# Encoder block on one core: earlier weights for the first two gates, and another PSUM bank for one fill

## Chip, core and metric

The kernel runs on one NeuronCore of one Trainium2 chip. The metric is the device time of one execution in microseconds (us). Five instruction streams run beside each other on the core and meet only at semaphores: PE (TensorE, matmuls), DVE (VectorE), ACT (ScalarE), POOL (GpSimd) and SP (SyncE, which issues most DMAs). PE writes its results to PSUM, which has 8 banks of 128 x 512 float32; DVE and ACT read them there. Everything else is in SBUF.

## What is computed

One encoder block over 1024 positions and 1024 channels, float32. From the normalised input come, by one projection, the queries, keys and values, two gate paths, and the inputs u and v of a gated MLP. Attention and MLP are two branches; each is projected back to 1024 channels, and two sigmoid gates made from the input weigh them against each other.

```python
h = rmsnorm(x, norm_gain)
z = jnp.einsum('bsd,de->bse', h, w_in)
q, k, v, gate_a, u_in, v_in, gate_b, g_merge = jnp.split(z, IN_SPLITS, axis=-1)
...
attn = block_attention(q, k, v) * jax.nn.silu(gate_a)
y_a = jnp.einsum('bse,ed->bsd', attn, w_proj_attn)
...
gm = u * v_mix.reshape(B, S, GMLP_WIDTH) * jax.nn.silu(gate_b)
y_b = jnp.einsum('bse,ed->bsd', gm, w_proj_gmlp)
g = jax.nn.sigmoid(g_merge.reshape(B, S, N_BRANCHES, D_MODEL) + b_merge)
y = g[:, :, 0, :] * y_a + g[:, :, 1, :] * y_b
return x + jnp.einsum('bsd,de->bse', y, w_out)
```

A final rmsnorm follows. There are 8 query heads and 2 key/value heads of 64, so the attention has 64 score tiles of 128 queries x 1024 keys.

## The kernel before

Most matrices are split into a high and a low part, and a product is three matmuls (high by high, high by low, low by high). A weight tile arrives by DMA ("wraw"), ACT makes the high part ("wh", line 110) and DVE or POOL the low part ("wl", line 116).

The order of the program is: keys and values; v of the MLP and its position mixing; queries; the attention with the remaining projections as filling work; the projection of the MLP branch, `proj_b`, here called the spatial projection (product "yb", eight output tiles `dt`); the eight pairs of merge gates `g0` to `g7` and, between them, the projection of the attention, `a0` to `a3`; the output projection.

The code is written in program order, without waits. A scheduler then sets the fixed order of each engine from that order and from when buffers come free, so a line that moves in the program can move instructions on every engine, and each engine runs its own list strictly in order. Buffers come from tags with a fixed number of slots: a new tile of a tag takes the slot of the oldest one and waits for its last reader. Three tags matter here. In PSUM there are three tiles of two banks ("S", for scores and large products), one bank "o" (`ps_o`) and one bank "z" (`ps_z`). In SBUF the tag "t2" (line 57) has four buffers of 128 x 512 float32.

The attention (lines 534 to 626). `scores` (line 545) makes a score tile on PE (s, lines 550 and 551), its negated maximum on DVE (nm, 553), the exponentials on ACT (P, 557), and splits the result into two float16 parts (p, ACT 563, DVE 564), which a transposing DMA turns (T, line 567). `mix` (line 569) multiplies the values with T in bank "o" (o, line 575); ACT and DVE add the halves (o2, line 578; og, 582). Between them stand the fills: 24 half tiles of the gate and u projections, of 24 matmuls each. Fill `fill_u` (507) has DVE read its bank (uw, line 511), then a tanh form of gelu (ut, 274 to 277), and POOL multiplies it into vm (514); `fill_a` (524) has DVE read it at line 494 (product ga, tile ga00w). `fill_bank` (line 503) chooses the bank of a fill: the n-th entry of `FB`, and "z" after that. The first two fills are u2's halves, `u20` and `u21`, the third is the first half of a0, `ga00`. Two of four groups of query transposes (qtp, line 349, copied by ACT at line 351 to qT) fall between the first fills, and those of rows 2 and 3 use "o" as well (`QTP`, line 354).

The gates (lines 666 to 720 and 807 to 832). `pair_weights` loads the weights of one gate pair ("graw", 1 MB), takes the squares of its four quarters on ACT (line 814; the squares themselves go to `junk`, which is bank "o"; their sums are kept), makes a scale of them (`unit_scale`, 666 to 675, with PE at 669, POOL at 673) and forms three sums on DVE (`sums`, 714 to 716, two of them in new tiles s1 and s2 of tag "t2"). `pair` then makes the product by seven instead of eight half products (`seven`, 683 to 711): "11", "21", "T2", "T3", "T1", "22", "T4", each with weights split by ACT (line 680) and DVE (681), 12 matmuls each into the first bank of a tile "S". The first product is copied by ACT to p1 (a "t2" tile, line 700), and DVE adds the others to it (696). The other operand are forms of the input (xf, from `x_chunk`) and, for `a0` to `a3`, of the attention (gf, gk), made by ACT and DVE at lines 110, 116 and 652.

`MORDER` (line 736) is the order of the last stage: "w" is `pair_weights`, "g" is `pair`, "a" a pair of output tiles of the attention's projection, "A" makes its forms.

Of the kernel before, what the change touches and what calls it, by code (L numbers as in the profile page):

```python
# [30 lines left out]
def hybrid_block_kernel(  # L31
# [30 lines left out]
    def junk(name):  # L62
        return ps_o(name)
# [13 lines left out]
    def ps_z(name):  # L77
        return ps.tile([P, 512], F32, tag="z", bufs=1, name=name)
# [99 lines left out]
    for i in range(4):  # L178
        for j in range(2):
            dt = 2 * i + j  # L180
# [11 lines left out]
            for tt in range(NT):  # L192
                o = kvb[tt // 2][:, 256 * (tt % 2):256 * (tt % 2) + 256]
# [303 lines left out]
        dve.scalar_tensor_tensor(out=t, in0=t, scalar=1.0, in1=w, op0=ALU.add, op1=ALU.mult)  # L497
        return t

    FB = (ps_z,)  # L500
    nfill = []

    def fill_bank(name):
        nfill.append(name)
        return FB[len(nfill) - 1](name) if len(nfill) <= len(FB) else ps_z(name)

# [124 lines left out]
    def proj_b(dt):  # L631
        yp = ps_s(f"yb{dt}")
        hi, lo = stream_w(W_PROJ + dt, 1, act, dve)
        for h in range(2):
            for et in range(4):
                mm3(yp[:, H(h)], hi[:, C(et)], lo[:, C(et)], gmh[:, et, H(h)], gml[et][:, H(h)], et == 0, et == 3)
        act.copy(ys[dt], yp)
# [95 lines left out]
    XLO = (dve, dve)  # L733
    XCS = (0, 1, 3, 5)
    EARLY = 2
    MORDER = "w0 g0 w1 g1 w2 A a0 g2 w3 g3 w4 a1 g4 w5 g5 w6 a2 g6 w7 a3 o g7"

    gk = []

# [12 lines left out]
    def load_chunk(j):  # L752
        for dt in (j, j + 4):
            xraw[dt] = t4(XT[j], f"xraw{dt}")
            nc.sync.dma_start(out=xraw[dt], in_=xT[C(dt), :])

    def x_chunk(j):
        q = {}
        for r in range(2):
            dt = j + 4 * r  # L760
            for h in range(2):
                t = q[r, h] = xraw[dt][:, None, H(h)]
                dve.scalar_tensor_tensor(out=xraw[dt][:, H(h)], in0=xraw[dt][:, H(h)], scalar=gs[:, dt:dt + 1],
                                         in1=rB[:, H(h)], op0=ALU.mult, op1=ALU.mult)

        def xf_tile(key, i):
            if not xfn:
                tag = XFT.pop(0)
                if tag == "ptr":
                    t = sb.tile([P, 4, 2, 1, 512], F16, tag="ptr", bufs=2, name=f"xf{key}{j}")  # L770
                else:
                    t = t4(tag, f"xf{key}{j}", F16, (P, 2048)).rearrange("p (n f k t) -> p n f k t", n=2, f=2, k=1)
                xfn.extend(t[:, n] for n in range(t.shape[1]))
            t = xfn.pop(0)
            return t[:, 0], t[:, 1]

        make_forms(q, 1, xf_tile, XB, XSUB, XHI, XLO)

    for j in range(2):
        load_chunk(j)  # L780
    for dt in range(8):
        proj_b(dt)
        if dt in XCS:
            j = XCS.index(dt)
            x_chunk(j)
            if j + 2 < 4:
                load_chunk(j + 2)

    def halves_of(t):
        return [t[:, H(0)], t[:, H(1)]]  # L790
# [16 lines left out]
    def pair_weights(dt):  # L807
        t = t8("qT", 4, f"graw{dt}", F32)
        nc.sync.dma_start(out=t[:, 0, :], in_=wall[W_TR + 20 + dt])
        nc.sync.dma_start(out=t[:, 1, :], in_=wall[W_TR + 12 + dt])  # L810
        a21, a22, a11, a12 = (t[:, k, H(h)] for k in range(2) for h in range(2))
        ss = small(f"gss{dt}", 4)
        for i, t in enumerate((a21, a22, a11, a12)):
            act.activation(junk(f"gsq{dt}{i}"), t, AF.Square, accum_out=ss[:, i:i + 1])
        sc = unit_scale(ss, 4, f"g{dt}")
        return sums(a11, a12, a21, a22, t2(f"s1{dt}"), t2(f"s2{dt}")), sc
# [20 lines left out]
        dve.tensor_tensor(out=ys[dt], in0=ys[dt], in1=ga, op=ALU.add)  # L837

    gates, GA, pws, yas = {}, {}, {}, {}
    yhl, who = {}, []  # L840

    wor, who4 = [], []
# [38 lines left out]

    for step in MORDER.split():
        i = int(step[1:] or 0)
# [149 lines left out]
```

## Time and profile before

| | us |
|---|---|
| median of 3 runs (lowest, highest) | 746.56 (745.75, 747.24) |
| the profiled execution | 744.79 |
| its span | 743.0 |
| PE busy | 712.1 |
| DVE busy | 596.4 |
| ACT busy | 446.8 |
| POOL busy | 97.2 |

The mean granted TensorE clock of the profiled execution is 0.988 of full speed. A row of the trace gives the start and duration of an instruction, its engine, line, operation and tiles, and in brackets how long its engine had nothing to do before it and which instruction ended that. Matmuls overlap, so their spacing is read from their starts. Where the chain of waits names several, it is the last to come.

### The profile page before, as it was taken

How to read it: one execution, taken by the hardware profiler on the slowest of the kernel's cores; microseconds unless marked ns; L12 is line 12 of the kernel's file. 1: busy time of each engine (PE TensorE's matmuls, PEld its weight loads, DVE VectorE, ACT ScalarE, POOL GpSimd, SP SyncE). 2: the span in 40 equal slices, each digit the busy share in tenths (PEclk: the TensorE clock that was granted, in tenths of full speed). 3: DMA queues.
4: the chain of work that ended last, by engine and by line, in shares of the span. 5: the costliest groups of instructions: out<-in, count | busy, mean ns of one | idle time of the engine just before them, and what ended most of it. 6: DMA issues, size and time to landing. Idle time of an engine off the chain costs nothing.

```text
span 743.0 us, 9814 instructions
## 1 busy us (share of the span) xinstructions
PE 712.1 (96%) x3561; PEld 530.1 (71%) x3561; DVE 596.4 (80%) x931; ACT 446.8 (60%) x775; POOL 97.2 (13%) x77
## 2 busy tenths in 40 slices
PE   8999999988999999999999995999999998999995
PEld 8978888766778888888878882455464555588884
DVE  5568988789798999988899999899888899934223
ACT  6646664676788898768787488555474446611101
POOL 0010242142121321232200002000000000000000
PEclk9999999989999999999999998999999999999998
DMA  8831301083769897898999800130031006241111
GB/s 309 301 100 36 114 15 42 1 142 78 136 128 181 166 179 142 162 177 157 166 234 323 183 16 1 56 128 15 18 125 57 0 1 231 109 142 68 46 58 56
DMA packets 152609, 85.47 MB, mean 115 GB/s; under 512 B 135408, under 2 KB 136048, under 8 KB 152560
## 3 DMA queue, kind: packets, MB, share of 16 engines
q1 hardware_dynamic: 152272, 84.56, 45.7%
q8 instruction: 28, 0.46, 0.3%
q10 hardware_dynamic: 288, 0.28, 0.1%
q14 instruction: 21, 0.17, 0.1%
HBM read 47.07 MB, written 4.19 MB: 69 GB/s over the span
## 4 chain that ended last, share of the span: by engine, by line
PE 81%; DVE 9%; DMA 4%; ACT 2%; issue 2%; POOL 1%; SPq 0%; POOLq 0%; DVEq 0%; ACTq 0%
PE o L575 6%; PE out L174 4%; PE out L173 4%; PE out L172 4%; DMA T<-p 3%; PE s L550 3%; PE s L551 3%; PE g L172 3%; PE g L174 3%; PE g L173 3%; PE q L172 2%; PE q L174 2%; PE v L172 2%; PE q L173 2%; PE v L173 2%; PE v L174 2%
## 5 line engine op out<-in xcount | busy, mean ns | idle before, releaser
L564 DVE SCALAR_TENSOR_TENSOR p<-P,ri,p 128x1024 f16<-128x1024 f32 x64 | 88.9, 1393 | 14.7 <-ACT p L563 14.3
L557 ACT ACTIVATE P<-s,nm 128x1024 f32<-128x1024 f32 x64 | 71.4, 1116 | 23.0 <-DVE nm L553 11.5
L553 DVE TENSOR_REDUCE nm<-s 128x1 f32<-128x1024 f32 x64 | 77.8, 1215 | 5.7 <-PE s L551 5.4
L563 ACT ACTIVATE p<-P,ri 128x1024 f16<-128x1024 f32 x64 | 72.8, 1143 | 14.7 <-DMA T<-p 11.3
L575 PE MATMUL o<-T,vS 128*128 128x256 f16 x512 | 61.8, 273 | 2.1 <-DMA T<-p 2.1
L575 PEld LDWEIGHTS <-vS 128*128 128x128 f16 x512 | 47.4, 98 | 16.0 <-issue 6.9
L550 PE MATMUL s<-kT,qT 128*128 128x512 f32 x128 | 53.0, 414 | 1.3 <-ACT P L557 1.3
L116 POOL TENSOR_TENSOR wl<-wraw,wh 128x512 fp32r<-128x512 f32 x24 | 36.0, 1504 | 111.6 <-ACT wh L110 96.2
L551 PE MATMUL s<-kT,qT 128*128 128x512 f32 x128 | 50.5, 395 | 0.0
L909 ACT ACTIVATE sq<-xr 128x1024 f32<-128x1024 f32 x7 | 7.4, 1061 | 61.5 <-DVE xr L963 61.5
L963 DVE TENSOR_TENSOR xr<-out,xr 128x1024 f32<-128x1024 f32 x7 | 8.6, 1225 | 44.0 <-PE out L174 43.9
L673 POOL TENSOR_TENSOR scg<-scg,mhalf 128x1 f32<-128x1 f32 x8 | 9.8, 1219 | 221.6 <-DVE scg L672 221.6
L110 ACT CAST wh<-wraw 128x512 fp32r<-128x512 f32 x35 | 21.5, 614 | 17.5 <-PE yb L173 7.5
L488 PE MATMUL ga<-xh,wh 128*128 128x512 f32 x64 | 26.5, 414 | 3.8 <-DVE uw L511 3.4
L550 PEld LDWEIGHTS s<-kT,qT 128*128 128x128 f32 x128 | 24.1, 188 | 6.7 <-ACT P L557 1.9
L551 PEld LDWEIGHTS s<-kT,qT 128*128 128x128 f32 x128 | 24.1, 188 | 4.9 <-issue 0.2
L488 PE MATMUL u<-xh,wh 128*128 128x512 f32 x64 | 25.6, 399 | 0.7 <-DVE ga01w L494 0.7
L490 PE MATMUL ga<-xh,wl 128*128 128x512 f32 x64 | 26.1, 407 | 0.0
L489 PE MATMUL ga<-xl,wh 128*128 128x512 f32 x64 | 26.0, 406 | 0.0
L680 ACT ACTIVATE wg<-graw,scg 128x512 f16<-128x512 f32 x16 | 11.4, 721 | 24.2 <-PE g L174 12.8
L172 PE MATMUL v<-nh,xh 128*128 128x512 f32 x64 | 25.5, 398 | 0.0
L174 PE MATMUL yb<-gmh,wl 128*128 128x512 f32 x64 | 25.5, 398 | 0.0
(557 smaller groups left out, 2158.5 us busy)
## 6 DMA issues: line engine op xcount, KB each, us to landing
wraw<-in_wall_dram SPq DMA_DIRECT2D x59, 256.0 KB, 3.2
graw<-in_wall_dram SPq DMA_DIRECT2D x16, 512.0 KB, 4.4
xraw<-in_xT_dram SPq DMA_DIRECT2D x15, 512.0 KB, 7.3
xn<-in_x_dram SPq DMA_DIRECT2D x8, 512.0 KB, 7.6
wor<-in_wall_dram SPq DMA_DIRECT2D x8, 512.0 KB, 4.9
xr<-in_x_dram SPq DMA_DIRECT2D x8, 512.0 KB, 5.1
out_dram<-xr SPq DMA_DIRECT2D x7, 512.0 KB, 2.6
T<-p SPq DMA_TRANSPOSE x64, 4.6
```

What stands on the lines that cost most here:

```text
L116: eng_lo.tensor_tensor(out=lo, in0=raw, in1=hi if hi.dtype == F16 else hi.bitcast(F32), op=ALU.subtract)
L172: pe.matmul(o, ah, bh, start=start, stop=False)
L173: pe.matmul(o, ah, bl, start=False, stop=False)
L174: pe.matmul(o, al, bh, start=False, stop=stop)
L488: pe.matmul(o, wh[:, C(dt % 4)], xh[dt][:, H(h)], start=(dt == 0), stop=False)
L550: pe.matmul(sp[:, H(hf)], qs, kT[:, 2 * v, H(hf)], start=True, stop=False)
L551: pe.matmul(sp[:, H(hf)], qs, kT[:, 2 * v + 1, H(hf)], start=False, stop=True)
L553: dve.tensor_reduce(out=nm, in_=sp, axis=AX.X, op=ALU.max, negate=True)
L557: act.activation(Pt, sp, AF.Exp, bias=nm, accum_out=rsum)
L563: act.activation(hi, Pt, AF.Copy, scale=ri)
L564: dve.scalar_tensor_tensor(out=lo, in0=Pt, scalar=ri, in1=hi, op0=ALU.mult, op1=ALU.subtract)
L575: pe.matmul(ot[:, 0:256], vS[:, kt, v, :], T[:, :, 8 * p + kt, :], start=(kt == 0 and p == 0), stop=(kt == 7 and p == 1))
```

## The change

Two edits. `FB` gets a second entry, so the second fill of the attention (`u21`) goes to bank "o" and the third (`ga00`) stays in "z". And `pair_weights` of the first two gate pairs is called inside the loop over the spatial projection, after `dt` 3 and `dt` 5, in place of "w0" and "w1" in `MORDER`; the loop moves below the functions for it. So the loads, squares, scales and sums of both pairs, with their "t2" tiles, come before the first `pair` in the program; before, those of the second pair came after the first `pair`. Lines 809 to 837 become 799 to 827 in the new file.

```diff
--- before.py
+++ after.py
@@ -497,7 +497,7 @@
         dve.scalar_tensor_tensor(out=t, in0=t, scalar=1.0, in1=w, op0=ALU.add, op1=ALU.mult)
         return t
 
-    FB = (ps_z,)
+    FB = (ps_z, ps_o)
     nfill = []
 
     def fill_bank(name):
@@ -733,7 +733,7 @@
     XLO = (dve, dve)
     XCS = (0, 1, 3, 5)
     EARLY = 2
-    MORDER = "w0 g0 w1 g1 w2 A a0 g2 w3 g3 w4 a1 g4 w5 g5 w6 a2 g6 w7 a3 o g7"
+    MORDER = "g0 g1 w2 A a0 g2 w3 g3 w4 a1 g4 w5 g5 w6 a2 g6 w7 a3 o g7"
 
     gk = []
 
@@ -776,16 +776,6 @@
 
         make_forms(q, 1, xf_tile, XB, XSUB, XHI, XLO)
 
-    for j in range(2):
-        load_chunk(j)
-    for dt in range(8):
-        proj_b(dt)
-        if dt in XCS:
-            j = XCS.index(dt)
-            x_chunk(j)
-            if j + 2 < 4:
-                load_chunk(j + 2)
-
     def halves_of(t):
         return [t[:, H(0)], t[:, H(1)]]
 
@@ -837,6 +827,18 @@
         dve.tensor_tensor(out=ys[dt], in0=ys[dt], in1=ga, op=ALU.add)
 
     gates, GA, pws, yas = {}, {}, {}, {}
+    for j in range(2):
+        load_chunk(j)
+    for dt in range(8):
+        proj_b(dt)
+        if dt in XCS:
+            j = XCS.index(dt)
+            x_chunk(j)
+            if j + 2 < 4:
+                load_chunk(j + 2)
+        if dt in (3, 5):
+            pws[dt // 4] = pair_weights(dt // 4)
+
     yhl, who = {}, []
 
     wor, who4 = [], []
```

Three places in the orders that result. First PE at the start of the attention, where the second group of query transposes, `qtp31`, stands (u21 is the second fill, ga00 the third, wh and wl the parts of their weights). Before:

```order
L490 MATMUL u21_1525<-xh7_334,wl161_1489 128x512
L349 MATMUL qtp31_1315<-identr_71,qs3_1305 128x128 [waits PE_49,Activation_49]
L349 MATMUL qtp31_1315<-identr_71,qs3_1305 128x128 x3
L488 MATMUL ga00_1889<-xh0_93,wh100_1879 128x512 [waits DVE_49]
L489 MATMUL ga00_1889<-xl0_94,wh100_1879 128x512
L490 MATMUL ga00_1889<-xh0_93,wl100_1880 128x512 [waits Pool_49]
```

and now:

```order
L490 MATMUL ga00_1889<-xh3_202,wl100_1880 128x512
L349 MATMUL qtp31_1315<-identr_71,qs3_1305 128x128 [waits PE_49,Activation_49]
L349 MATMUL qtp31_1315<-identr_71,qs3_1305 128x128 x3
L488 MATMUL u21_1525<-xh0_93,wh160_1482 128x512 [waits PE_49,Activation_49]
L489 MATMUL u21_1525<-xl0_94,wh160_1482 128x512
L490 MATMUL u21_1525<-xh0_93,wl160_1483 128x512
```

The second fill stood ahead of the transposes and the third fill behind them; now 12 matmuls of the third fill stand ahead, and the second fill behind, with a wait for ACT.

Then DVE at the same place, around the instruction that reads the second fill's bank (uw21, line 511; uw20 and ut20 belong to the first fill, nm and p16 to score tiles, qs to the queries). Before:

```order
L330 TENSOR_TENSOR qst2_1271<-qst2_1271,qtmp2_1558 128x1024 [waits DVE_49]
L560 RECIPROCAL ri010_1437<-ri010_1437 128x1 [waits Activation_49]
L277 SCALAR_TENSOR_TENSOR ut20_1519<-ut20_1519,uw20_1517 128x512 [waits Activation_49]
L511 TENSOR_TENSOR uw21_1550<-u21_1525,rB_1373 128x512 [waits PE_49]
L553 TENSOR_REDUCE nm020_1467<-s020_1462 128x1
L341 TENSOR_TENSOR qs4_1573<-qst2_1271,qs4_1573 128x8x64 [waits Activation_49]
```

and now:

```order
L330 TENSOR_TENSOR qst2_1271<-qst2_1271,qtmp2_1558 128x1024 [waits DVE_49]
L277 SCALAR_TENSOR_TENSOR ut20_1519<-ut20_1519,uw20_1517 128x512 [waits Activation_49]
L553 TENSOR_REDUCE nm020_1467<-s020_1462 128x1 [waits PE_49]
L564 SCALAR_TENSOR_TENSOR p16010_1440<-P010_1434,ri010_1437,p16010_1440 128x1024 [waits DMAHW4_49,Activation_49]
L560 RECIPROCAL ri011_1455<-ri011_1455 128x1 [waits Activation_49]
L341 TENSOR_TENSOR qs4_1573<-qst2_1271,qs4_1573 128x8x64 [waits Activation_49]
L341 TENSOR_TENSOR qs5_1589<-qst2_1271,qs5_1589 128x8x64 [waits PE_49,Activation_49]
L511 TENSOR_TENSOR uw21_1550<-u21_1525,rB_1373 128x512 [waits PE_49]
L311 TENSOR_REDUCE qf3_1776<-qtmp3_1774 128x16 [waits Activation_49]
```

One maximum, one low part of p and two low parts of the queries stand now ahead of that read.

Last ACT at the start of the gates, from the copy of the first product of gate 0, p1g0, on (wg are the parts of gate weights, gsq20 and gsq21 squares of the third gate pair). Before:

```order
L700 COPY p1g0_4605<-g011_4609 128x512 [waits PE_49]
L680 ACTIVATE wg0T3_4658<-graw0_4578,scg0_4592 128x512 [waits Activation_49]
L110 CAST gfT30_4920<-gat0_1919 128x1024 [waits DVE_49]
L110 CAST xfT31_4321<-xraw5_4212 128x512 [waits DVE_49]
L680 ACTIVATE wg0T1_4675<-s10_4598,scg0_4592 128x512 [waits PE_49]
L680 ACTIVATE wg022_4693<-s20_4599,scg0_4592 128x512 [waits DVE_49,PE_49]
L680 ACTIVATE wg0T4_4711<-graw0_4578,scg0_4592 128x512 [waits DVE_49,PE_49]
L680 ACTIVATE wg111_4757<-graw1_4729,scg1_4743 128x512 [waits DVE_49,PE_49,Pool_49]
L680 ACTIVATE wg121_4774<-graw1_4729,scg1_4743 128x512 [waits DVE_49,PE_49]
L814 ACTIVATE gsq20_4884,gss2_4883<-graw2_4880 128x512 [waits DMAHW5_49]
```

and now:

```order
L680 ACTIVATE wg0T1_4700<-s10_4445,scg0_4439 128x512 [waits PE_49]
L680 ACTIVATE wg022_4718<-s20_4446,scg0_4439 128x512 [waits DVE_49,PE_49]
L700 COPY p1g0_4630<-g011_4634 128x512 [waits DVE_49]
L804 ACTIVATE gsq20_4884,gss2_4883<-graw2_4880 128x512 [waits DMAHW5_49]
L804 ACTIVATE gsq21_4886,gss2_4883<-graw2_4880 128x512 [waits Activation_49]
L680 ACTIVATE wg0T4_4736<-graw0_4425,scg0_4439 128x512 [waits PE_49]
L804 ACTIVATE gsq22_4888,gss2_4883<-graw2_4880 128x512 [waits DMAHW6_49,Activation_49]
L804 ACTIVATE gsq23_4890,gss2_4883<-graw2_4880 128x512 [waits Activation_49]
```

The copy waits for DVE instead of PE, and stands behind the weights of T1 and of "22"; two squares of the third pair stand ahead of the weights of T4, where they stood behind the first two of gate 1.

## Rows read from the trace of the kernel before

**Rows 1.** The page's busy times (with share of the span and number of instructions), and PE's row of slices: 40 slices of 18.6 us, busy share in tenths.

```profile
PE 712.1 (96%) x3561; PEld 530.1 (71%) x3561; DVE 596.4 (80%) x931; ACT 446.8 (60%) x775; POOL 97.2 (13%) x77
...
PE   8999999988999999999999995999999998999995
```

**Rows 2.** Stretches of the span: its bounds and length, busy time of PE, PE's weight loads, DVE, ACT and POOL with their number of instructions, granted TensorE clock, DMA share and GB/s.

```profile
140.00:220.00 80.00, 71.82 (x376) 57.66 (x375) 70.72 (x98) 57.84 (x115) 21.19 (x13) 0.96 0.59 107
220.00:360.00 140.00, 140.00 (x760) 113.71 (x759) 127.67 (x184) 114.71 (x203) 34.73 (x25) 1.00 0.89 166
440.00:460.00 20.00, 12.37 (x48) 7.62 (x47) 19.50 (x34) 17.89 (x36) 1.54 (x1) 0.83 0.00 0
480.00:620.00 140.00, 140.00 (x649) 76.19 (x647) 123.33 (x214) 74.43 (x133) 3.68 (x6) 1.00 0.14 49
620.00:640.00 20.00, 17.82 (x79) 9.63 (x78) 19.63 (x26) 12.60 (x17) 0.00 (x0) 1.00 0.68 263
```

**Rows 3.** PE in order of time at the start of the attention (start, duration, engine, line, operation, tiles, shape; in brackets the idle time before it and what ended it).

```profile
147.05 0.46 PE L349 MATMUL qtp<-identr,qs 128*128 128x128 f32 x4
...
152.90 0.46 PE L349 MATMUL qtp<-identr,qs 128*128 128x128 f32 x4
156.76 0.80 PE L488 MATMUL ga<-xh,wh 128*128 128x512 f32 x1 [3.40 <-DVE uw L511]
...
162.43 0.40 PE L489 MATMUL ga<-xl,wh 128*128 128x512 f32 x1
```

**Rows 4.** DVE in order of time, the same stretch.

```profile
146.58 1.27 DVE L564 SCALAR_TENSOR_TENSOR p<-P,ri,p 128x1024 f16<-128x1024 f32 x1
...
151.38 1.92 DVE L564 SCALAR_TENSOR_TENSOR p<-P,ri,p 128x1024 f16<-128x1024 f32 x1
...
154.43 1.68 DVE L277 SCALAR_TENSOR_TENSOR ut<-ut,uw 128x512 f32<-128x512 f32 x1
156.03 0.68 DVE L511 TENSOR_TENSOR uw<-u,rB 128x512 f32<-128x512 f32 x1
```

**Rows 5.** POOL in order of time, the same stretch.

```profile
150.92 1.30 POOL L116 TENSOR_TENSOR wl<-wraw,wh 128x512 fp32r<-128x512 f32 x1 [8.12 <-ACT wh L110]
153.61 1.94 POOL L116 TENSOR_TENSOR wl<-wraw,wh 128x512 fp32r<-128x512 f32 x1 [1.40 <-ACT wh L110]
```

**Rows 6.** Short stretches in the two idle times (columns as in rows 2).

```profile
156.00:158.00 2.00, 1.24 (x3) 1.05 (x4) 2.00 (x4) 2.00 (x3) 1.28 (x1) 0.50 1.16 182
...
454.00:456.00 2.00, 0.69 (x3) 0.61 (x4) 1.55 (x4) 1.82 (x5) 1.09 (x1) 0.50 0.00 0
```

**Rows 7.** ACT in order of time: the two copies of a group of query transposes.

```profile
153.44 0.64 ACT L351 CAST qT<-qtp 128x256 fp32r<-128x256 f32 x2
```

**Rows 8.** PE in order of time, later in the attention.

```profile
183.36 1.91 PE L575 MATMUL o<-T,vS 128*128 128x256 f16 x16 [1.45 <-DMA T<-p]
185.96 0.50 PE L488 MATMUL u<-xh,wh 128*128 128x512 f32 x1 [0.69 <-DVE ga01w L494]
...
193.51 0.54 PE L349 MATMUL qtp<-identr,qs 128*128 128x128 f32 x4 [1.41 <-ACT qT L351]
...
200.56 0.47 PE L550 MATMUL s<-kT,qT 128*128 128x512 f32 x1
```

**Rows 9.** PE in order of time at the start of the gates ("usg" is the sum of squares; from 455.90 on gate 0, from 477.52 on gate 1).

```profile
454.48 0.59 PE L669 MATMUL usg<-gss,mhalf 128*128 128x4 f32 x2 [5.67 <-ACT gsq L814]
455.90 0.61 PE L172 MATMUL g<-xf,wg 128*128 128x512 f16 x1 [0.82 <-ACT wg L680]
...
459.34 0.38 PE L173 MATMUL g<-xfT,wg 128*128 128x512 f16 x1
...
465.60 0.38 PE L174 MATMUL g0T<-xfT,wg0T 128*128 128x512 f16 x1
467.58 0.39 PE L174 MATMUL g0T<-xf,wg0T 128*128 128x512 f16 x1 [1.61 <-DVE wg0T L681]
...
469.75 0.38 PE L172 MATMUL g0T<-xf,wg0T 128*128 128x512 f16 x1
...
477.52 0.38 PE L172 MATMUL g<-xf,wg 128*128 128x512 f16 x1
```

**Rows 10.** DVE in order of time, gate 0.

```profile
455.12 0.16 DVE L674 RECIPROCAL scg<-scg 128x1 f32<-128x1 f32 x1 [0.45 <-POOL scg L673]
...
468.65 0.68 DVE L716 TENSOR_TENSOR graw<-graw 128x512 f32<-128x512 f32 x1
...
470.63 0.74 DVE L681 SCALAR_TENSOR_TENSOR wg<-s,scg,wg 128x512 f16<-128x512 f32 x1
471.29 1.22 DVE L116 TENSOR_TENSOR gfT<-gat,gfT 128x1024 fp32r<-128x1024 f32 x1
472.43 0.68 DVE L715 TENSOR_TENSOR s<-s,graw 128x512 f32<-128x512 f32 x1
473.03 0.74 DVE L681 SCALAR_TENSOR_TENSOR wg0T<-graw,scg,wg0T 128x512 f16<-128x512 f32 x1
```

**Rows 11.** ACT in order of time, gate 0.

```profile
461.26 0.59 ACT L700 COPY p1g<-g 128x512 f32<-128x512 f32 x1
...
475.81 0.60 ACT L814 ACTIVATE gsq<-graw 128x512 f32<-128x512 f32 x1
```

**Rows 12.** The DMAs issued from 466 to 480: number, KB each, median time from issue to landing.

```profile
graw<-in_wall_dram SPq DMA_DIRECT2D x2, 512.0 KB, 3.7
```

## The prediction

> **What bounds the kernel now.** I read the busy shares first, then the slices, then stretches, then the engine's rows in order of time. PE (TensorE) is busy 712.1 us of the 743.0, DVE (VectorE) 596.4 [rows 1]; so the time is PE's work plus the few places where PE stands, and an edit is worth only what it does to these. The row of slices shows where: a 5 in the middle of a row of nines, some eights before it, and the ends [rows 1]. The stretches give their sizes [rows 2]: PE lacks 8.2 us of 80 between 140 and 220, 7.6 us between 440 and 460, 2.2 us between 620 and 640. Between 220 and 360 and between 480 and 620 it is busy to the last hundredth, so what is won or lost before such a stretch is still there behind it. The change touches the first place (start of the attention) and the second (start of the gates). The profiled execution took 744.79 us, 1.79 more than its span and 1.77 less than the median of 746.56; the sum is made against 744.79 and then lifted by 1.77.
>
> **First place, the fill's bank.** Today both fills of u2 and the first of a0 use the bank "z". PE finishes the second fill, transposes at 152.90, and then cannot begin a0 (ga) before DVE has read the bank (uw, line 511): 3.40 us idle [rows 3]. DVE's read starts only at 156.03, because it stands behind two instructions that were stretched, 1.92 us at 151.38 where the same kind takes 1.27 at 146.58, and 1.68 us at 154.43 where a pass of that size takes 0.68 [rows 4]; beside both, POOL (GpSimd) was making low parts of weights [rows 5]. After the idle time the granted clock is 0.50 and matmuls start 0.43 us apart: the 13 of them from 156.76 to 162.43 take 5.67 us, where 13 at 0.23 take 2.99 [rows 3, 6]. So 2.68 us more.
>
> With the second fill in bank "o", PE runs 12 matmuls of ga straight behind the transpose of 147.05, then the other transposes, then the second fill. What is new is a wait in front of that fill: bank "o" held the transposes, and ACT (ScalarE) must copy them out. In the trace such a pair of copies started at 153.44 and took 0.64 us, right after the transposes of 152.90 [rows 3, 7]; with issue and queue I put 1.0 us, bounds 0.3 and 2. Behind it stands the fill itself, then the first mix o, which now needs DVE to have read bank "o". In the new DVE order that read stands behind one more maximum, a low part of p and two low parts of q; by the steps below (1.14, 1.2, 0.6, 0.6) that is 3.6 us more than before, and without the two stretchings (0.65 and 1.00) it ends near 158.6, where PE arrives from 157.1 on with two transposes and two matmuls still to do. So a wait of under a microsecond there.
>
> Sum: 3.40 + 2.68 gone, 1.0 new. The later idles of 1.45, 0.69 and 1.41 us [rows 8] wait for transposed probabilities (T), for DVE and for ACT; with the work before them earlier some of that goes and some comes back, as PE arrives earlier too. I keep 0.4 of it as gain. Term: -5.5 us; bounds 0 (all found again as other waits, since DVE is busy 70.7 of 80 us there [rows 2]) and -8 (3.40, 2.68 and half of the 3.55).
>
> **Second place, the gates.** Loads, squares, scales and sums of gates 0 and 1 are now asked for during the spatial projection. The first question is what this moves. The squares of a pair write to bank "o" too, and the new order leaves them in the same place on ACT behind the last mix's reads: so the idle of 5.67 us and of 0.82 us ahead of gate 0 [rows 9] stays. DVE gets gate 1's sums earlier. In the trace they ran among gate 0's steps, the last two at 468.65 (line 716) and 472.43 (715) [rows 10]; now they come before gate 0's scale. Two of them stand in front of it in a stretch where DVE is busy 19.50 of 20 us [rows 2], less what is taken from there: gate 0 starts 0.6 us later.
>
> The second question is what the earlier allocation costs. The pool "t2" has four buffers. Before, gate 1's sums were allocated after gate 0's copy p1; now s10, s20, s11 and s21 are all alive when p1 is wanted, so p1 takes the buffer of s10, whose last reader is the low part of gate 0's T1 weights (line 681). So ACT's copy of line 700, which ran at 461.26 [rows 11], waits for DVE. Its instruction also frees the bank of product "11", and the fourth product, T3, needs that bank. Behind it on ACT wait the squares of gate 2 and the high part of T4; on DVE, the additions that need p1.
>
> When? DVE's steps are taken from starts of consecutive rows [rows 10]: 0.66 for a low part (470.63 to 471.29), 1.14 for a pass of 1024 columns (to 472.43), 0.60 for one of 512 (to 473.03). From the reciprocal of gate 0's scale, 455.12 before and 455.75 with the 0.6, to the end of T1's low part the new order has eight short passes (4.80), four long ones (4.56), five low parts (3.30) and five of one column (together 0.42): 13.08, so 468.83. With ACT's copy, 0.6, T3 can start at 469.45. PE, which starts gate 0 near 456.4, has the three products before it done near 466.1 (today 465.60 plus 0.22 [rows 9], and 0.5 later): idle 3.3 us. Today it waits here too, 1.61 us until 467.58, with two matmuls of T3 already behind it, and T1 starts at 469.75. Then: T3 469.45, twelve at 0.216 us, T1 at 472.05, so 2.3 us late. Gate 2's squares stand now ahead of T4's high part: gate 2's load is issued after gfT's pass, landing 3.7 us later [rows 12], two squares of 0.75 (475.81, [rows 11]) and T4's parts end near 477, when PE wants them at 477.2. Nothing more from it, at most 0.8.
>
> The idle of 3.3 us may cost clock. The rows: 3.40 us idle was followed by 0.50, 5.67 us too, 1.61 was not [rows 3, 6, 9]. The nearest row is 3.40, so I count it, at the price of the gates' own matmuls: from 455.90 to 459.34 eight starts took 3.44 us where 0.216 each makes 1.73 [rows 9]: 1.7 us; bounds 0 and 2.7. Term: 2.3 + 1.7 = +4.0; bounds -1 (DVE runs ahead at once, since gate 1's sums no longer stand in this stretch) and +6.
>
> From there to 620 nothing waits [rows 2], so the difference stays; at 620 DVE is the late one (19.63 of 20) and a small shift of PE neither adds nor gives much: 0, bounds -1 and +1.
>
> Together: -5.5 + 4.0 = -1.5, 743.3 for an execution like the profiled one, **745.1 us** against the median.
>
> **Rivals.**
> *The second place costs nothing (741).* p1 waits, but PE finds T3 ready in time because DVE, relieved of three sums (1.8 us) inside the stretch, reaches T1's low part earlier, and the clock stays up. For it: the bounds above, and that DVE's list there is long and was placed by a scheduler. Against it: the count of 13.08 us already leaves those sums out. Then -5.5: 744.79 - 5.5 + 1.77 = 741.1.
>
> *The read of bank "o" is late (749.4).* The place is the first mix; it decides if POOL's low parts of weights again fall beside DVE's chain in front of uw. Then DVE has the 3.6 us more and also the 1.65 us of stretching: the read ends at 160.3, PE stands from 157.5, 2.8 us, close to the 3.40 that cost 2.68 in clock. Of the 5.5 us there remain 5.5 - 1.65 - 2.68 = 1.2, and with the second place's +4.0 the kernel is 2.8 us slower: 749.4. For it: POOL has the same three instructions in this stretch in the new order, one of them moved ahead of the weights' low parts; DVE has no slack before 160. Against it: ACT's casts that feed POOL come later than before, behind the low parts in question.
> The row shows a DVE pass that ends 0.56 us after POOL's instruction of 153.61 ends (155.55), as if it had only then begun. The Trainium skill ("SBUF — State Buffer", section "SBUF: two separate sides") says that GpSimd and a VectorE operation with two SBUF inputs share a pair of ports as an exclusive lock, held for the whole instruction, so that the later one stands until it is free. This trace agrees, with 1.68 us for a pass of 0.68. By that rule every overlap costs DVE up to the whole POOL instruction, 1.3 to 1.9 us, and this rival is the likelier the more of the three fall in front of uw.
>
> *No net change (746.6).* The gain at the first place is given back inside the attention (from 360 to 400 PE lacks time again, and ACT's and DVE's orders change throughout), and the second place is hidden.
>
> **Chances.** Forecast 0.45, its own range 743 to 748; second place free 0.20; late read 0.25; no net change 0.10. A difference below 0.2% (1.5 us) can't be told from none here. Faster: 0.24 of the forecast's 0.45 (it lies at that limit), 0.20 and 0.01, so 0.45. Same: 0.18, 0.02 of the late read, 0.08, so 0.28. Slower: 0.27. Eight in ten: 740.5 to 750.5, from just under the free case to just over the late one.
>
> **What would show it.** First place: the idle of 3.40 ahead of ga is gone and the granted clock stays at 1.00 from 150 to 164; an idle of about 1 us ahead of the second fill, ended by ACT's copy of qtp; the scores that start at 200.56 [rows 8] start near 195. Second place: gate 0 still behind an idle of some 5 to 6 us ended by ACT's squares; the copy of line 700 for gate 0 starts after a DVE low part of line 681, 12 to 14 us after gate 0's first weights; an idle of about 3.3 us in front of T3, ended by that copy, with clock 0.50 behind it; gate 1 about 2.5 us earlier than 477.5 if the first gain arrives whole, less the clock. Wrong if T3 starts without a wait, or if PE stands 2 us or more in front of the first mix.

## The result, and the profile after

The changed kernel takes 747.71 us (median of 20 runs, 745.65 to 749.83), the kernel before, in the same comparison, 745.51 us (20 runs): ratio 1.0029, 95% interval 1.0019 to 1.0040. It is slower by 2.2 us, where 1.5 us faster was forecast; 747.71 lies inside the range. Where one execution of a kernel took far longer than its others (807 to 2549 us), it is left out of that kernel's median.

The profiled execution took 747.99 us, with a span of 746.2. Every engine runs the same instructions in the same order up to the attention in both, but the first score tile began at 135.74 us before and at 137.74 after: 2.0 us between two executions, not between two kernels. So stages are compared from that tile on.

The page's busy times and PE's slices of the changed kernel, as in [rows 1]:

```profile
PE 713.9 (96%) x3561; PEld 528.8 (71%) x3561; DVE 594.8 (80%) x931; ACT 446.5 (60%) x775; POOL 95.5 (13%) x77
...
PE   8999999999899999999999995899999998999995
```

The first place answers as forecast. Stretches of the changed kernel (columns as in [rows 2]):

```profile
140.00:160.00 20.00, 18.76 (x93) 14.97 (x92) 18.12 (x28) 14.60 (x31) 4.58 (x3) 1.00 0.28 53
456.00:458.00 2.00, 0.70 (x2) 0.13 (x2) 1.62 (x5) 1.48 (x3) 0.49 (x1) 0.50 0.00 0
468.00:472.00 4.00, 1.62 (x8) 0.78 (x8) 4.00 (x6) 1.12 (x2) 0.00 (x0) 1.00 0.00 0
```

and PE in order of time in the first of them:

```profile
152.19 0.46 PE L349 MATMUL qtp<-identr,qs 128*128 128x128 f32 x4
153.54 0.50 PE L488 MATMUL u<-xh,wh 128*128 128x512 f32 x1 [0.90 <-ACT qT L351]
...
159.63 0.53 PE L349 MATMUL qtp<-identr,qs 128*128 128x128 f32 x4 [0.34 <-DVE qs L341]
```

The idle of 3.40 us and the clock of 0.50 behind it [rows 3, 6] are gone; in their place stands the wait for ACT's copies, 0.90 us. But what PE wins here it gives back inside the attention. The next rows are stretches that begin 0, 112, 147 and 215 us behind the first score tile (columns as in [rows 2]). Before:

```profile
135.74:175.74 40.00, 36.04 (x172) 28.88 (x171) 33.55 (x49) 28.74 (x58) 12.12 (x7) 0.91 0.45 79
...
247.74:282.74 35.00, 35.00 (x191) 28.49 (x190) 34.44 (x49) 31.11 (x55) 8.18 (x7) 1.00 0.87 162
282.74:315.74 33.00, 33.00 (x178) 26.80 (x177) 30.75 (x46) 26.61 (x47) 6.69 (x5) 1.00 0.88 160
...
350.74:385.74 35.00, 34.28 (x183) 27.56 (x182) 31.30 (x48) 27.08 (x47) 5.52 (x4) 1.00 0.97 194
```

and after:

```profile
137.74:177.74 40.00, 38.35 (x201) 30.71 (x200) 36.46 (x54) 29.00 (x59) 13.60 (x7) 1.00 0.43 86
...
249.74:284.74 35.00, 33.65 (x179) 26.73 (x178) 31.77 (x48) 28.23 (x50) 8.46 (x5) 1.00 0.82 151
284.74:317.74 33.00, 32.59 (x176) 26.19 (x175) 28.50 (x43) 25.59 (x47) 8.64 (x6) 1.00 0.81 165
...
352.74:387.74 35.00, 33.47 (x181) 26.60 (x179) 30.70 (x46) 26.61 (x48) 4.35 (x4) 1.00 1.01 201
```

In the first 40 us PE runs 201 instructions instead of 172. From 112 us on it runs 179, 176 and 181 where it ran 191, 178 and 183, and it now stands idle in the first two of these, where it stood nowhere before. DVE, busy 34.44 of 35 us there before, is busy 31.77 after: it waits more too. One of PE's waits, followed back through rows in order of time of POOL, SP's queue, DVE, ACT and PE:

```profile
262.65 2.38 POOL L116 TENSOR_TENSOR wl<-wraw,wh 128x512 fp32r<-128x512 f32 x1 [6.44 <-ACT wh L110]
...
265.06 4.47 SPq L120 DMA_DIRECT2D wraw<-in_wall_dram  x2
269.69 10.55 SPq L567 DMA_TRANSPOSE T<-p  x4
...
262.61 1.27 DVE L564 SCALAR_TENSOR_TENSOR p<-P,ri,p 128x1024 f16<-128x1024 f32 x1
263.80 1.78 DVE L277 SCALAR_TENSOR_TENSOR ut<-ut,uw 128x512 f32<-128x512 f32 x1
...
275.75 1.28 DVE L564 SCALAR_TENSOR_TENSOR p<-P,ri,p 128x1024 f16<-128x1024 f32 x1 [1.71 <-ACT p L563]
...
274.56 1.15 ACT L563 ACTIVATE p<-P,ri 128x1024 f16<-128x1024 f32 x1 [1.92 <-DMA T<-p]
277.12 1.11 ACT L557 ACTIVATE P<-s,nm 128x1024 f32<-128x1024 f32 x1 [1.41 <-DVE p L564]
...
278.38 0.51 PE L550 MATMUL s<-kT,qT 128*128 128x512 f32 x1 [0.98 <-ACT P L557]
```

Read from below: a score tile (s) waits for its buffer, which ACT's exponentials P free; ACT waits for DVE's low part of p; DVE for ACT's high part; that for a buffer which a transpose (T) reads; and the transposes start at 269.69, though the p of 262.61 was ready at 263.9, because SP's queue holds two weight loads ahead of them, whose buffers POOL reads (to 265.03, and again from 266.89 to 269.18). Before, SP waited so for POOL 10.4 us in 7 places between 220 and 390 us, after 21.3 us in 8; PE's wait for P occurred once there (0.7 us), after five times (3.3 us).

POOL's reading takes long itself: 2.38 us, where the same instruction took 1.30 at 150.92 [rows 5]; and DVE's pass of 263.80 took 1.78, where its size takes 0.68. POOL's ends 1.15 us after DVE's pass of 262.61 does, and DVE's 0.55 us after POOL's, as if each had begun only when the other ended. The Trainium skill ("SBUF — State Buffer", section "SBUF: two separate sides") describes an exclusive lock on a pair of ports that GpSimd shares with a VectorE operation of two SBUF inputs, held for a whole instruction; these rows agree with it.

The second place: PE in order of time at the gates, after (to be held against [rows 9]):

```profile
455.28 0.59 PE L669 MATMUL usg<-gss,mhalf 128*128 128x4 f32 x2 [6.57 <-ACT gsq L804]
457.30 0.61 PE L172 MATMUL g<-xf,wg 128*128 128x512 f16 x1 [1.43 <-ACT wg L680]
...
470.38 0.38 PE L172 MATMUL g0T<-xf,wg0T 128*128 128x512 f16 x1 [2.60 <-ACT p1g L700]
...
472.96 0.38 PE L172 MATMUL g0T<-xf,wg0T 128*128 128x512 f16 x1
```

with the two rows of DVE and ACT that stand in front of T3 (now p1's copy, 461.26 in [rows 11], begins when DVE's low part of T1 has read the buffer):

```profile
468.96 0.75 DVE L681 SCALAR_TENSOR_TENSOR wg0T<-s,scg,wg0T 128x512 f16<-128x512 f32 x1
...
469.74 0.59 ACT L700 COPY p1g<-g 128x512 f32<-128x512 f32 x1 [1.21 <-DVE wg0T L681]
```

The wait is where it was forecast, 2.60 us long. Stages of both kernels and of the experiments on their parts, in us, worked out from starts of PE's matmuls (first score tile; 17th score tile; the 61st matmul of line 172 in the spatial projection, called its end; gate 0's first; T1's first; gate 1's first of a T product):

| kernel | first score to 17th | first score to end of projection | end to gate 0 | gate 0 to T1 | T1 to gate 1 | ratio |
|---|---|---|---|---|---|---|
| before | 78.39 | 309.30 | 10.86 | 13.85 | 12.95 | |
| after | 73.76 | 308.32 | 11.24 | 15.66 | 13.09 | 1.0029 |
| e1_fill_bank | 73.59 | 308.61 | 7.78 | 13.91 | 13.80 | 0.9942 |
| e4_first_pair | 73.77 | 307.86 | 7.78 | 13.91 | 13.80 | 0.9953 |
| e16_sums_late | 73.72 | 308.72 | 7.78 | 13.91 | 13.80 | 0.9968 |
| e3_p1_apart | 73.71 | 307.17 | 11.70 | 12.08 | 12.95 | 0.9977 |

After, 4.63 us are won at the 17th tile, 0.98 of them are left at the end of the projection, and the gates cost 2.33. Between the 17th tile and that end PE's idle times come to 3.61 us in six places after and to 1.58 in three before: 2.03 of the 3.65 us that are lost.

One profile is one execution. But ten kernels here run the attention in the changed kernel's order on PE, DVE, ACT and POOL (after, and e1, e3, e4, e7, e8, e11, e14, e15 and e16 below). Against the one profile of before, all ten have won 4.57 to 4.95 us at the 17th tile, and 0.11 to 2.13 are left at the end of the projection.

### The profile page after: what moved, and what is told of

It reads as the page before. It is cut to its first block, busy times and chain, and to the rows that moved or that the text cites. A ratio compares the mean times of both kernels' runs of the same rounds, so it can differ in the third digit from the quotient of the medians.

```text
span 746.2 us, 9806 instructions
## 1 busy us (share of the span) xinstructions
PE 713.9 (96%) x3561; PEld 528.8 (71%) x3561; DVE 594.8 (80%) x931; ACT 446.5 (60%) x775; POOL 95.5 (13%) x77
## 4 chain that ended last, share of the span: by engine, by line
PE 72%; DVE 11%; ACT 6%; DMA 5%; issue 3%; POOL 1%; SPq 0%; POOLq 0%; ACTq 0%; DVEq 0%
DMA T<-p 4%; PE out L174 4%; PE out L173 4%; PE out L172 4%; PE o L575 4%; PE g L172 3%; PE g L174 3%; PE g L173 3%; DVE p L564 2%; ACT p L563 2%; PE s L550 2%; PE q L172 2%; PE q L174 2%; PE v L173 2%; PE v L172 2%
## 5 line engine op out<-in xcount | busy, mean ns | idle before, releaser
L564 DVE SCALAR_TENSOR_TENSOR p<-P,ri,p 128x1024 f16<-128x1024 f32 x64 | 85.6, 1344 | 18.9 <-ACT p L563 18.5
L557 ACT ACTIVATE P<-s,nm 128x1024 f32<-128x1024 f32 x64 | 71.4, 1116 | 22.6 <-DVE p L564 10.3
L116 POOL TENSOR_TENSOR wl<-wraw,wh 128x512 fp32r<-128x512 f32 x24 | 39.0, 1629 | 108.1 <-ACT wh L110 75.5
L673 POOL TENSOR_TENSOR scg<-scg,mhalf 128x1 f32<-128x1 f32 x8 | 6.3, 785 | 223.1 <-DVE scg L672 223.1
L110 ACT CAST wh<-wraw 128x512 fp32r<-128x512 f32 x35 | 21.3, 613 | 13.6 <-PE sp L173 3.6
L488 PE MATMUL gb<-xh,wh 128*128 128x512 f32 x64 | 25.5, 399 | 0.0
L174 PE MATMUL v<-nh,xl 128*128 128x512 f32 x64 | 25.4, 396 | 0.0
L172 PE MATMUL q<-nh,xh 128*128 128x512 f32 x64 | 25.2, 394 | 0.0
```

The source lines that it names most:

```text
L116: eng_lo.tensor_tensor(out=lo, in0=raw, in1=hi if hi.dtype == F16 else hi.bitcast(F32), op=ALU.subtract)
L172: pe.matmul(o, ah, bh, start=start, stop=False)
L174: pe.matmul(o, al, bh, start=False, stop=stop)
L488: pe.matmul(o, wh[:, C(dt % 4)], xh[dt][:, H(h)], start=(dt == 0), stop=False)
L557: act.activation(Pt, sp, AF.Exp, bias=nm, accum_out=rsum)
L564: dve.scalar_tensor_tensor(out=lo, in0=Pt, scalar=ri, in1=hi, op0=ALU.mult, op1=ALU.subtract)
```

## The experiments

Sixteen kernels ran. Of e2_weights and e13_late_square only the times are used, not the traces.

**The parts one by one.** The bank alone (before, with one line changed), the weights alone (after, with that line put back), p1 of gate 0 in a buffer of its own, and the bank with the first pair's weights alone early:

```diff
 e1_fill_bank, from before
-    FB = (ps_z,)
+    FB = (ps_z, ps_o)
 e2_weights, from after
-    FB = (ps_z, ps_o)
+    FB = (ps_z,)
 e3_p1_apart, from after
-        p1 = t2(f"p1{name}")
+        p1 = sb.tile([P, 512], F32, tag="wraw", bufs=4, name=f"p1{name}") if name == "g0" else t2(f"p1{name}")
 e4_first_pair, from after
-    MORDER = "g0 g1 w2 A a0 g2 w3 g3 w4 a1 g4 w5 g5 w6 a2 g6 w7 a3 o g7"
+    MORDER = "g0 w1 g1 w2 A a0 g2 w3 g3 w4 a1 g4 w5 g5 w6 a2 g6 w7 a3 o g7"
...
-        if dt in (3, 5):
+        if dt == 3:
```

> The second fill in bank "o" alone; the weights as before. Theory A (the gain at the start of the attention is given back inside the attention, to the softmax chain): PE is about 5 us ahead at 220 and about 0.6 us ahead at the end of the spatial projection, and the kernel takes 0.6 us less, ratio 0.997 to 1.001. Rival B (the gain lasts, and the changed kernel lost it at the gates): 5 us less, ratio 0.993.

Measured: 742.10 us, ratio 0.9942 (0.9920 to 0.9964).

> The earlier weights alone; both first fills in bank "z". Theory A: the copy p1 of gate 0 waits for the buffer of s10, PE stands 2.6 us in front of T3, and the kernel is 2.5 us slower, ratio 1.002 to 1.005. Rival B (the earlier weights cost all that the fill wins): 7 us slower, ratio 1.009. Rival C (the weights cost nothing): ratio 1.000.

Measured: 746.84 us, 1.0014 (0.9998 to 1.0031).

> Both edits, but the copy p1 of gate 0 has a buffer of the weight tiles' tag in place of one of "t2", so that it waits for nobody. Theory A: no idle of 2.6 us ended by p1, T3 waits at most 1.6 us for its own low part as before; about 2.5 us less than the changed kernel, ratio to before 0.997 to 1.001. Rival (the loss at the gates comes from gate 0 starting later and from the order of squares): still 1.002 or more.

Measured: 744.83 us, 0.9977 (0.9963 to 0.9991). ACT copies p1 at 462.80 without a wait, between gate 0's first matmul and T1 PE stands 0.22 us at most in one place, and T1 starts 12.08 us behind gate 0 instead of 15.66.

> Both edits, but only the first pair's weights move into the loop; the second pair's come after gate 0 as before, so four "t2" buffers suffice. Theory A: no wait for p1, ratio to before 0.997 to 1.001. Rival (any move of the weights costs): 1.002 or more.

Measured: 742.82 us, 0.9953 (0.9933 to 0.9973).

What follows: the bank is worth 3.9 us alone, the weights alone cost 0.9 or nothing, and both together cost 2.2: the parts don't add. p1's buffer is worth 2.9 us of medians (3.4 with each taken against before in its own comparison). The harm lies with the second pair's weights: in e4_first_pair every engine runs the same list, by operation, tile name and shape, as in e1_fill_bank, so moving the first pair changed nothing there. The table shows something not forecast too: the bank alone has won only 0.69 us when the projection ends, and 2.17 more at the gates, where gate 0 starts 7.78 us behind the projection instead of 10.86. The steps of DVE there tell why, below.

**Why the first gain is lost: the transposes.** If the transposes' traffic sets the attention's pace, half of it should free PE. Before, and the bank alone, with only the high parts of p transposed, and used by the mix in place of the low ones too:

```diff
-        nc.sync.dma_start_transpose(T16[j, qt][:, h], p16)
+        nc.sync.dma_start_transpose(T16[j, qt][:, h, 0:8], hi)
...
-                pe.matmul(ot[:, 0:256], vS[:, kt, v, :], T[:, :, 8 * p + kt, :],
+                pe.matmul(ot[:, 0:256], vS[:, kt, v, :], T[:, :, kt, :],
```

> The kernel before with one half left out: only the high float16 part of the probabilities is transposed, and the mix reads it twice, so a transposing DMA moves half as much; all else runs. Control for the next run. Theory A (the transposes hold the softmax chain in the attention): ACT's waits for T between 220 and 400 (9.7 us) nearly vanish. Time within 4 us below the kernel before, since PE is the bound there.

> The same left out, with the second fill in bank "o". Theory A: PE's waits for ACT's P (3.2 us between 220 and 400 with the bank alone) vanish, and the end of the spatial projection comes 4 to 5.5 us earlier against the control, each from its own first score tile, in place of 0.7 to 1.0. Rival (DVE's or ACT's own work is what gives the gain back): still about 1 us.

Measured: 741.98 us, 0.9964 (0.9950 to 0.9978), and 746.71, 1.0016 (1.0005 to 1.0027). The median time from issue to landing falls from 4.6 and 4.4 us to 3.2 in both, and ACT still waits for transposes 10.8 and 11.2 us between 220 and 400 (9.7 before, and 12.8 after, whose attention has the order of the bank alone). The two go apart: the first is faster than before, the second slower than the bank alone by 4.6 us. The edit also gives PE, DVE and ACT another order. So it speaks against the traffic as the limit, and settles no more.

**The same: the queue.** If it is the weight loads ahead of the transposes in SP's queue, the loads of the fills should go to POOL's queue. The bank alone, and before, with:

```diff
-        nc.sync.dma_start(out=raw, in_=wall[i, :, H(half)])
+        (nc.gpsimd if W_TR <= i < W_TR + 12 else nc.sync).dma_start(out=raw, in_=wall[i, :, H(half)])
```

> The second fill in bank "o" alone, and the weight tiles of the attention's fills are loaded from POOL's queue in place of SP's, so that no transposing DMA stands behind a load that waits for its buffer. Theory D (the gain is given back because transposes on SP stand behind such loads: one took 4.47 us while two finished tiles stood behind it): PE's waits for ACT's P between 214 and 388 fall from 3.2 to under 1.5 us, and the end of the spatial projection comes 2 to 4 us earlier against the bank alone, each from its first score tile; ratio to before 0.988 to 0.992. Rival (ACT's and DVE's own work sets the pace of the attention): PE's waits stay near 3 us, ratio 0.993 to 0.996.

> The kernel before with the same loads from POOL's queue: control. Theory D: PE had only 0.7 us of waits for P there, so at most 1 us less, ratio 0.998 to 1.001; the 3.40 us of the first place stay. Rival: loads from POOL cost DVE time by themselves, 1.002 or more.

Measured: 744.93 us, 1.0001 (0.9979 to 1.0023), and 746.92, 1.0023 (1.0003 to 1.0043). PE in order of time in e9_pool_loads:

```profile
178.80 0.50 PE L550 MATMUL s<-kT,qT 128*128 128x512 f32 x1 [0.21 <-ACT P L557]
182.16 2.33 PE L575 MATMUL o<-T,vS 128*128 128x256 f16 x16 [2.16 <-DVE qst L330]
202.08 1.91 PE L575 MATMUL o<-T,vS 128*128 128x256 f16 x16 [0.21 <-DMA T<-p]
```

Between 214 and 379 us PE waits no more for P (0.39 us remain, at 379.21). But another wait of 2.16 us stands at 182.16 and one of 2.19, for a transpose, at 216.35; the projection ends 309.13 us behind the first score tile (308.61 for the bank alone), and gate 0 starts 10.87 us behind it, as before. So nothing was gained over the bank alone. Nor does the run single out the queue, for the scheduler's order went back too: PE runs 1304 matmuls between the first score tile and the projection's first in both of these kernels, as before, and 1328 in after and with the bank alone.

Held against its control, the run shows something else. Each counted from its own first score tile, the 17th tile starts 3.28 us earlier in e9_pool_loads than in e10_pool_before, the 19th to the 62nd 3.06 to 3.08 us earlier, and the projection ends 2.64 us earlier. Here, nearly in before's order and with the loads off SP's queue, the lead lasts through the stretch in which the changed kernel loses it. Which of the two keeps it is not shown. Moving the loads has a price of its own: in e10_pool_before the projection ends at 311.77, 2.47 us later than before, in one execution each.

**Squares earlier.** Squares go to bank "z" in place of "o", so they need not stand behind the last mix. After; after with p1 apart; the bank alone; and that with the loads on POOL's queue as well:

```diff
-        return ps_o(name)
+        return ps_z(name)
```

> Both edits, with the squares written to bank "z", which is free after the last fill, in place of "o". Theory A (DVE is the bound at the gates, and p1 hangs on its list): gate 0 starts some 6 us earlier behind the projection, but p1 and T3 come hardly earlier, so T3's idle grows to 7 us or more, and the kernel stays within 1.5 us of the changed one, ratio to before 1.001 to 1.005. Rival (the idle in front of gate 0, 6.57 and 1.43 us, is what counts): 6 to 8 us less than the changed kernel, ratio 0.992 to 0.995.

> As the run before, and p1 of gate 0 in a buffer of the weight tiles' tag. Theory A: no wait for p1; PE follows the low parts that DVE makes; a little better than with p1 apart alone (0.9977), 0.993 to 0.998. Rival (the bank of the squares doesn't matter once DVE is full): 0.9977 as there.

> The second fill in bank "o" and the squares in bank "z", the program's order of the weights as in the kernel before (second pair behind gate 0). Theory A for the gates (p1's buffer and the second pair's squares in front of gate 0 are the price, not the early squares): gate 0 starts right behind the projection, p1 waits for nobody, and the kernel is 1 to 4 us faster than with the bank alone, ratio 0.989 to 0.993. Rival (DVE's list is the bound, whoever stands first): as the bank alone, 0.994.

> The run before with the fills' loads from POOL's queue. If both theories hold the gains add: ratio 0.984 to 0.989. Rival: what the attention wins is lost behind DVE at the gates, ratio as the run before.

Measured: 746.37 us, 1.0016 (1.0001 to 1.0031); 745.66, 1.0001 (0.9987 to 1.0015); 745.26, 0.9996 (0.9977 to 1.0015); 746.48, 1.0008 (0.9990 to 1.0027). PE at gate 0 in e7_squares_z:

```profile
456.47 0.59 PE L173 MATMUL g0T<-xfT,wg0T 128*128 128x512 f16 x1 [3.61 <-DVE xfT L116]
464.61 0.59 PE L172 MATMUL g0T<-xfT,wg0T 128*128 128x512 f16 x1 [3.72 <-ACT xfT L110]
```

Gate 0 starts 2.09 us behind the projection instead of 11.24, and T1 22.48 behind gate 0 instead of 15.66: 9.15 us earlier, 6.82 of them given back before T1. PE now waits for the forms of the input (xfT), which DVE and ACT make; DVE is busy without a gap from 449 to 464 us, and ACT waits for DVE there (5.01 us before its cast of 459.52). Behind both waits the granted clock is 0.50 (456.5 to 459, 464.7 to 467), which is part of what is given back. So the wait for ACT's squares at 455.28 names what comes last, not what limits; these rows point to DVE's list. With the bank alone the same edit costs 3.2 us (745.26 against 742.10), where 1 to 4 were expected to be won: gate 0 starts 2.08 us behind the projection, but gate 1's T product 37.83 instead of 35.49.

**What holds gate 0 back.** One theory was the last square of the second pair, which ACT took ahead of gate 0's weights. It is tied to gate 0's scale, so that it comes later (before; after; after with p1 apart):

```diff
+            if dt == 1 and i == 3:
+                zb = small("zb")
+                dve.tensor_scalar(out=zb, in0=scs[0][:, 0:1], scalar1=0.0, scalar2=None, op0=ALU.mult)
+                act.activation(junk(f"gsq{dt}{i}"), t, AF.Square, bias=zb, accum_out=ss[:, i:i + 1])
+            else:
...
+        sc = scs[dt] = unit_scale(ss, 4, f"g{dt}")
```

> The kernel before, where the fourth square of the second pair is tied to gate 0's scale (its bias is zero times that scale), so that it can't stand ahead of gate 0's weights on ACT, nor its sum ahead of gate 0 on PE. The attention's order is untouched. Theory E (the place of the second pair's last square and sum, not the fill's bank, is what made the run with the bank alone fast at the gates): gate 0 starts 3 us earlier behind the projection, gate 1 two; ratio to before 0.995 to 0.999. Rival (the fill's bank made that gain): 1.000.

> Both edits and the same tie. Theory E: gate 0 starts about 3 us earlier than in the changed kernel, but p1 still waits for s10's buffer, so the idle in front of T3 grows by about as much; ratio to before 1.000 to 1.003. Rival (p1's wait follows gate 0's start): 3 us less than the changed kernel, 0.997 to 0.999.

> Both edits, the tie, and p1 of gate 0 in a buffer of the weight tiles' tag: both causes taken away with both edits in place. Theory E: as the bank alone or the first pair alone, ratio to before 0.993 to 0.997. Rival (the second pair's earlier sums on DVE cost by themselves): 0.998 or more.

Measured: 744.52 us, 0.9989 (0.9974 to 1.0005); 747.36, 1.0030 (1.0014 to 1.0045); 745.45, 0.9999 (0.9987 to 1.0011). In e14_late_after ACT takes the square at 458.84, behind gate 0's first weights, and yet gate 0 starts 11.24 us behind the projection, as in after; in e15_late_apart it starts 12.31 behind. That theory fell.

What was left are the sums of the second pair on DVE. They alone are put back behind gate 0; the pair's loads, squares and scale stay early:

```diff
+        if dt == 1:
+            return (a11, a12, a21, a22), sc
         return sums(a11, a12, a21, a22, t2(f"s1{dt}"), t2(f"s2{dt}")), sc
...
     def pair(dt, w, sc):
+        if dt == 1:
+            w = sums(*w, t2(f"s1{dt}"), t2(f"s2{dt}"))
```

> The changed kernel, with one part put back: gate 1's loads, squares and scale stay in the spatial projection, but its three sums (and their two "t2" tiles) are taken behind gate 0, as before. Theory S (the sums cost all: two of their passes stand in DVE's full list ahead of gate 0's scale, and their tiles take p1's buffer): gate 0 starts 7.8 us behind the end of the projection instead of 11.2, T1 13.9 us behind that instead of 15.7, and the kernel is like the one with the first pair alone: 742.8, ratio 0.995. Theory Q (gate 1's loads and squares themselves hold gate 0 back): gate 0 stays at 11.2 to 11.7, T1 at 12 as with p1 in a buffer of its own, and the time is 744.8, ratio 0.998.

Measured: 742.97 us, 0.9968 (0.9955 to 0.9980), and the stages 7.78 and 13.91 of the bank alone to the hundredth. DVE in order of time from the first step of gate 0's scale (line 671) to the second (672), after:

```profile
451.71 0.15 DVE L671 TENSOR_REDUCE scg<-usg 128x1 f32<-128x4 f32 x1
451.79 1.28 DVE L116 TENSOR_TENSOR xfT<-xraw,xfT 128x512 f16<-128x512 f32 x2
452.99 1.22 DVE L116 TENSOR_TENSOR gk<-gat,gk 128x1024 fp32r<-128x1024 f32 x1
454.12 0.68 DVE L716 TENSOR_TENSOR graw<-graw 128x512 f32<-128x512 f32 x1
454.72 0.14 DVE L672 TENSOR_SCALAR scg<-scg 128x1 f32<-128x1 f32 x1
```

and in e16_sums_late:

```profile
451.13 0.16 DVE L671 TENSOR_REDUCE scg<-usg 128x1 f32<-128x4 f32 x1
451.20 0.68 DVE L116 TENSOR_TENSOR xfT<-xraw,xfT 128x512 f16<-128x512 f32 x1
451.80 0.15 DVE L672 TENSOR_SCALAR scg<-scg 128x1 f32<-128x1 f32 x1
```

The scale's tiny steps are links of a chain (DVE, POOL, DVE; ACT's weights hang on it) in a list without gaps. After, four passes stand between two links, 3.01 us; here one, 0.67. One of the four is a sum of the second pair; the others were ordered around it. That is 2.34 of the 3.46 us by which gate 0 is later; the first link itself comes 1.03 us later behind the projection. The sums' early place costs 4.50 us from the projection's end to gate 1 (39.99 against 35.49), and 4.7 us of medians (747.71 against 742.97). The loads and squares cost nothing because they did not move: by operation, tile name (without its number) and shape, every engine runs the same list in e16_sums_late as in e1_fill_bank, and SP issues the same DMAs in the same order. Of the second edit only the second pair's sums, with their tiles, have any effect beside the bank edit, and e1, e4 and e16 are three measurements of one order (742.10, 742.82, 742.97).

## Why the prediction was wrong

The direction was wrong: 1.5 us faster was forecast, 2.2 slower measured. By its own steps:

- **First place, at its place: right.** The forecast was -5.5, measured -4.63 at the 17th score tile. The idle and the slow clock are gone, the new wait took 0.90 us (forecast 1.0), and PE did not stand in front of the first mix, so the rival of the late read fell.
- **The step that failed: "Between 220 and 360 and between 480 and 620 it is busy to the last hundredth, so what is won or lost before such a stretch is still there behind it."** It held from 480 on: from gate 1's T product to the last matmuls the kernels in the table differ by 0.14 us at most. In the attention it did not: of 4.63 us, 0.98 are left at the end of the projection. The prediction took the stretch from the kernel before, but the changed kernel does not run it: the bank edit gives PE, DVE and ACT another order there, and in it PE waits for P where [rows 2] shows no idle time. The chain of one such wait is shown above. Why the lead is lost stays open. Either the new order costs it, or PE, moved forward, met suppliers that had been just ahead of it (a DVE busy for 91% of [rows 2], transposes behind weight loads in SP's queue). No run here separates the two. That a lead need not be lost there, e9_pool_loads shows against its control: 2.64 of 3.28 us were left. The rival "no net change" named this half of the outcome, with a chance of 0.10.
- **Second place, p1's buffer: right in mechanism and size.** From gate 0 to T1 the working gave 472.05 - 456.4 = 15.65 us; measured 15.66 (472.96 - 457.30). That is no accident: from the reciprocal (456.52) to the end of T1's low part DVE ran the passes that were counted, 13.10 us by the next start (469.62) for 13.08. The idle in front of T3 was 2.60 us for 3.3, because PE reached T3 later: the first three products took 10.3 us for 9.7, with eleven matmuls at the low clock for eight. Gate 0 starts 0.38 us later, for 0.6.
- **The clock behind T3's wait: wrong.** +1.7 us was counted from the nearest row, 3.40 us of idle time. After 2.60 us the granted clock stayed at 1.00 (468 to 472), the level of 2.4 GHz, and matmuls started 0.22 us apart. So the second place came to +2.33 us and not +4.0.
- **The sum.** -0.98 and +2.33 give +1.35; to the output projection's last matmul of line 172 the profiles give +1.20 (599.90 us from the first score tile against 598.70), the medians +2.2. The last microsecond is not placed: single executions of one kernel lie that far apart.
- **What the sum left out.** The three sums were priced as 1.2 us of passes in front of gate 0. Against before that looked right. But the bank edit alone brings gate 0 forward by 3.08 us, by another order on DVE and ACT, and the early sums keep the changed kernel from it. A price against before can't show a gain that is blocked.

The version with the bank edit alone beats both kernels: 742.10 us, 0.9942 of before. Against it, and not against before, the second edit costs 4.50 us at the gates.

## What to carry to other kernels

A PE without idle time over a long stretch does not prove that an early gain is still there behind it: look whether the edit changes the engines' orders in that stretch, and how far ahead of PE its suppliers are. Before work is moved forward, count what it asks of an engine whose list is full, and whose buffers its tiles take; here three short sums and their two tiles did the harm. A line that moves in the program need not move on an engine: the loads and squares didn't. And try the parts of an edit alone: here one was worth 3.9 us and the other took it away.

## What was not expected of the hardware

An idle time of 2.60 us in front of T3 left the granted clock at 1.00, where 3.40 us in [rows 3] was followed by 0.50; at the start of the gates, 6.57 and 1.43 us of waiting were followed by 0.50 (456 to 458), and in e7_squares_z 3.61 and 3.72 us were too.

A transpose of half the width landed in 3.2 us instead of 4.4 to 4.6 (median from issue to landing): half the bytes took about 0.7 of the time.
